# A transformer block with rotating weight tiles: first projection's conditioning blocks in pairs, and a longer delay before a conditioning row's columns are used

## The chip, the core and the metric

The kernel runs on one core of a Trainium2 chip. The metric is the device time of one execution in microseconds (us). TensorE (PE) multiplies, VectorE (DVE) and ScalarE (ACT) work on rows, GpSimd (POOL) and SyncE (SP) issue transfers.

## The reference

The network has two parts in a row on one sequence of 256 tokens with 1024 channels: two layers (attention with an MLP, a recurrent block with an MLP), and behind them a block with three mixers and a mixture of experts. Each sub-layer's input and output are modulated by a conditioning vector `c`. The part that the change touches is the first modulation and the projection behind it:

```python
def ada_modulation(c, w, b):
    mod = jax.nn.silu(c) @ w + b
    shift, scale, gate = jnp.split(mod, 3, axis=-1)
    return shift[:, None, :], scale[:, None, :], gate[:, None, :]
...
        shift, scale, gate = ada_modulation(c, ada_w[i, 0], ada_b[i, 0])
        h = x * (1.0 + scale) + shift
        if i % N_MIXERS == 0:
            y = windowed_gqa(h, attn_w_in[j], attn_w_out[j], attn_sinks[j])
...
        x = layer_norm(DN_ALPHA * x + (1.0 + gate) * y, ln_g[i, 0], ln_b[i, 0])
```

All inputs are float32. `c` is one row of 1024, and each conditioning weight is 1024 by 3072, so a conditioning product is a row times a matrix, and most of its cost is reading the matrix.

## The kernel before, in words

**The stream of weights.** All large matrices of the kernel pass through one list of items, `W` (class `Stream`, L136 on). Each item is a tile of up to 1 MB. Five buffers rotate (`NSTAGE`), SP issues the transfers in the list's order (`load_to`, L194), and an item's buffer is free when its reader is done. There are two kinds of items. A weight (`add`) is split into a high and a low float32r part before use, 1024 columns at a time: ScalarE writes `wh` (L219), VectorE the remainder `wl` (L224); `mm3` (L389 to L393) then multiplies three times, high by high, and each low by the other's high. A filler (`fill`) is a tile of a conditioning matrix with a function that uses it. `W.step()` advances by one item, `W.next(tag)` runs fillers until it comes to the named weight, and `W.drain()` runs the fillers up to the next weight. Each step also issues loads for the next five items and splits for the next weight.

**Orders.** TensorE's instructions in the attention are issued in the order in which the program writes them (`manual_schedule`). The other engines' orders are made when the program is built: an operation goes in when its inputs are reckoned ready, and among those that are ready the one that the program wrote first goes first. On the chip each engine works in its fixed order and waits at an operation whose inputs are late.

**The first projection** (`project`, L1087 to L1119) runs over eight chunks of 128 input channels. For each chunk the weight's 128 rows of 1536 columns are one item ("attn_in", 768 KB, runs of 6 KB), and 18 matmuls add this chunk to six accumulators: keys and values for two halves of the tokens (6 matmuls, two buffers of `gen`, a pool of three, L404) and queries (12 matmuls, `acc`). The chunk's input has to be modulated first. Its 128 shifts and 128 scales come from one filler: `ada0(c)` (L660) reads 1024 rows of two stretches of 128 columns, in runs of 512 bytes, 1 MB in all; eight matmuls (`cS` has silu(c) in one column of 32, L673) leave partial rows in four groups of PSUM partitions, and VectorE copies them to `adaR` (L675). `modulate(c)` (L1075) turns them into two columns with matmuls by a column of ones (L1079, into a buffer of `gen`), VectorE adds the bias (`ab`, L1081), ScalarE scales and shifts the chunk (`v`, L1083), and VectorE splits it into hH and hL (L1084, L1085). In the list blocks and weights alternate. Within chunk c the order is: weight c, the product of block c+1, keys and values of c, `modulate(c + 1)`, queries of c. Behind some chunks stands a piece of another computation (`next(hy)`, the long filters of the second part).

**Rows to columns.** The shifts and scales of the later modulations are made from rows too, but go through memory: `row_cols` (L487) writes the row to DRAM (`flat`, L491) and reads it back as columns (`adaC`, L492), both on POOL's queue, and puts the function that uses the columns on a list with a count of `LAG`:

```python
        GP.dma_start(flat, R[row:64 * n:32, :])
        GP.dma_start(C[:, :n, :], flat.rearrange("(s r) (p k) -> s (r p) k", s=n, k=8).rearrange("s p k -> p s k"))
        W.due.append([LAG, lambda: use(C)])
```

Every `step` begins with `wait_less` (L252), which counts the list down by one and runs a function whose count is below 0. So with `LAG = 2` the function's operations are written at the third step after `row_cols`, with 4 at the fifth. The normalisation behind a sub-layer (`post`, L1350) runs whatever is still listed. The functions are `use` in `ada1` (L571 to L575, operations on `sst` and `ab`) for three modulations, and in `ada2` (L601 to L603, and L610) for the second part.

**The attention's end.** There the first of these rows is finished, and beside it the gate of the attention, whose matrix is four fillers that VectorE multiplies (`adav`, L466 and L468, two operations each). The steps behind `row_cols` are: two gate fillers, the third output weight, two gate fillers, the fourth output weight. Then `gate_sums` (L507) sums the gate over partitions with matmuls into `gen` (L504) and VectorE adds them to the gate (L505). Then come the last products of probabilities and values (`ov`, L1192) and the output projection.

Of the kernel before, what the change touches and what calls it, by code (L numbers as in the profile page):

```python
# [11 lines left out]
F32 = mybir.dt.float32  # L12
# [3 lines left out]
OP = mybir.AluOpType  # L16
# [17 lines left out]
GROUPS = [(0,), (1, 2), (3, 4), (5, 6)]  # L34
RANK = [0, 6, 7, 8, 9, 2, 3, 1, 4, 5, 10, 11, 12, 13]
NSTAGE, NPART, NMORE = 5, 4, 6
LAG = 2
QSCALE = float(HD ** -0.5)


# [94 lines left out]
class Stream:  # L135
# [124 lines left out]
    def next(self, tag, ahead=None):  # L260
        while True:
            got = self.step(ahead)
            if got is not None:
                assert got[0] == tag, (got[0], tag)
                return got[1]
# [15 lines left out]
def tile_model(ctx: ExitStack, tc: tile.TileContext, A, out):  # L281
    nc = tc.nc
    PE, V, SC, GP = nc.tensor, nc.vector, nc.scalar, nc.gpsimd
# [4 lines left out]
    sml = ctx.enter_context(tc.tile_pool(name="sml", bufs=2))  # L288
    rows = ctx.enter_context(tc.tile_pool(name="rows", bufs=4, space=bass.MemoryType.DRAM))

    W = Stream(tc, stage, parts, NSTAGE, 1)
# [14 lines left out]
    def K(name):  # L306
        o, n = OFF[name]
        return csm[:, o:o + n]

    ident = K("ident")  # L310
    one = K("ones")
# [14 lines left out]
    cS = cst.tile([128, 8, 32], F32, name="cS")  # L326
# [6 lines left out]
    csil = cst.tile([128, 3, 8], F32, name="csil")  # L333
# [55 lines left out]
    def mm3(o, a, b, first, last):  # L389
        (ah, al), (bh, bl) = a, b  # L390
        PE.matmul(o, ah, bh, start=first, stop=False)  # L391
        PE.matmul(o, ah, bl, start=False, stop=False)  # L392
        return PE.matmul(o, al, bh, start=False, stop=last)  # L393
# [5 lines left out]
    psC = pes.enter_context(tc.tile_pool(name="psC", bufs=1, space=PSUM))  # L399

    def accb():
        return psA.tile([128, 512], F32, name="acc")

    def gen():  # L404
        return psB.tile([128, 512], F32, name="gen")
# [8 lines left out]
    def finish(job=None):  # L414

        if job is not None:
            FIN["jobs"].append(job)
        if job is None or not FIN["keep"]:
            while FIN["jobs"]:
                FIN["jobs"].pop(0)()  # L420

    def ada_fill(key, cs, wv, c0, n, fin, bank=None, biases=None):
# [4 lines left out]
        def step(kc, last):  # L427
            def fn(t):
# [8 lines left out]
                if last:  # L437
                    R = sml.tile([128, 512], F32, name="adaR", bufs=1)
                    if biases:
                        V.tensor_add(R[:, :n], st["ps"][:, :n], biases())  # L440
                    else:
                        V.tensor_copy(R[:, :n], st["ps"][:, :n])
                    finish(lambda: fin(R))
            return fn
# [32 lines left out]
    def sum_rows(acc, n):  # L477

        ps = gen()
        for g in range(2 * n):  # L480
            PE.matmul(ps[32 * g:32 * g + 32, :], one.to_broadcast([128, 32]), acc[:, 512 * g:512 * g + 512],
                      start=True, stop=True)
        R = sml.tile([128, 512], F32, name="adaR", bufs=1)
        SC.activation(R[:64 * n, :], ps[:64 * n, :], AF.Copy)
        return R

    def row_cols(R, row, n, use):  # L487
# [4 lines left out]
        GP.dma_start(C[:, :n, :], flat.rearrange("(s r) (p k) -> s (r p) k", s=n, k=8).rearrange("s p k -> p s k"))  # L492
        W.due.append([LAG, lambda: use(C)])

# [63 lines left out]
    def biases():  # L558
        return MOD["b5"]
# [76 lines left out]
    def rview(name, idx):  # L636
        return A[name][idx].rearrange("(m p) n -> p m n", p=128)
# [17 lines left out]


    ADA0 = {}
    VCH = ()

    def ada0(c):  # L660
        def fn(t):
            tv = t.rearrange("p (j n) -> p j n", j=8)
            if c in VCH:
                R = sml.tile([128, 256], F32, name="adaQ")
                V.tensor_scalar(R, tv[:, 0, :], csil[:, 0, 0:1], None, op0=OP.mult)
                for j in range(1, 8):
                    V.scalar_tensor_tensor(R, tv[:, j, :], csil[:, 0, j:j + 1], R, op0=OP.mult, op1=OP.add)
                ADA0[c] = R
                return
            ps = psC.tile([128, 512], F32, name="adaps")  # L670
            for j in range(8):
                g = j % 4
                PE.matmul(ps[32 * g:32 * g + 32, :256], cS[:, j, :], tv[:, j, :], start=(j < 4), stop=(j >= 4))  # L673
            R = sml.tile([128, 512], F32, name="adaR", bufs=1)
            V.tensor_copy(R[:, :256], ps[:, :256])  # L675
            ADA0[c] = R

        ap = A["ada_w"][0, 0][:, 0:2048].rearrange("(p j) (s c n) -> c p j s n", j=8, s=2, n=128)[c]
        W.fill("ada", ap, fn)

    wv, wo = rview("attn_w_in", 0), rview("attn_w_out", 0)
    for k in range(8):
        ada0(k)
        W.add("attn_in", wv[:, k, :])
    fl = collect([ADA1[0, 1][0], ADA1[0, 0][3]])
    for m in range(4):
# [354 lines left out]
    def attention():  # L1041
        aes = ExitStack()
        ap = aes.enter_context(tc.tile_pool(name="attn", bufs=1, reuse_waits="tile"))
# [13 lines left out]
        def turn_in(first):  # L1057
            for b in (0,) if first else (1, 2, 3):
                pt = accb()
                for k in range(2):  # L1060
                    for t in range(2):
                        c = 2 * b + k
                        PE.transpose(pt[:, 256 * k + 128 * t:256 * k + 128 * t + 128],
                                     x_nat[:, t, 128 * c:128 * c + 128], ident)
                (SC.copy if b % 2 else V.tensor_copy)(xT[:, 2 * b:2 * b + 2, :],
                                                      pt.rearrange("p (k n) -> p k n", k=2))
            if not first:
                return
            pt = gen()
            PE.transpose(pt[:, 0:16], brow, ident[:16, :16])  # L1070
            pv = pt[:, 0:16].rearrange("p (s k) -> p s k", s=2)
            V.tensor_copy(badd[:, 0], pv[:, 0])
            V.tensor_scalar(badd[:, 1], pv[:, 1], 1.0, None, op0=OP.add)

        def modulate(c):  # L1075
            R = ADA0.pop(c)
            ps = gen()
            for s in range(2):
                PE.matmul(ps[:, s:s + 1], R[:, 128 * s:128 * s + 128], one, start=True, stop=True)  # L1079
            ab = sml.tile([128, 2], F32, name="ab0")  # L1080
            V.tensor_add(ab, ps[:, 0:2], badd[:, :, c])  # L1081
            v = ip.tile([128, 256], F32, name="v0", bufs=2)
            SC.activation(v, xT[:, c, :], AF.Identity, bias=ab[:, 0:1], scale=ab[:, 1:2])  # L1083
            V.tensor_copy(hH[:, c, :], v)  # L1084
            V.tensor_sub(hL[:, c, :], v, hH[:, c, :].bitcast(F32))  # L1085

        def project(hy):  # L1087
            W.step()
            turn_in(True)
            kv = [gen(), gen()]  # L1090
            modulate(0)
            
            qa = [[accb(), accb()], [accb(), accb()]]
            for c in range(8):
                w = W.next("attn_in")
                (qh, ql), (kh, kl) = w.parts

                def rows(ps, t, wh, wl):
                    ts = slice(128 * t, 128 * t + 128)
                    mm3(ps, (hH[:, c, ts], hL[:, c, ts]), (wh, wl), c == 0, c == 7)  # L1100

                if 0 < c < 7:
                    W.step()
                for t in range(2):
                    rows(kv[t], t, kh, kl)
                if c == 0:
                    turn_in(False)
                    W.step()
                if c < 7:
                    modulate(c + 1)  # L1110
                for g in range(2):
                    sl = slice(512 * g, 512 * g + 512)
                    for t in range(2):
                        rows(qa[g][t], t, qh[:, sl], ql[:, sl])
                for _ in range((0, 1, 0, 0, 1, 1, 1, 1)[c]):
                    next(hy)
                if c == 6:
                    nc.sync.dma_start(amask, A["c_amask"])
            return kv, qa  # L1119
# [90 lines left out]

        hy = hy_filters()
        ps, qa = project(hy)
        ies.close()
        aw = aes.enter_context(tc.tile_pool(name="attw", bufs=2, reuse_waits="tile"))
        ADP["pool"] = aes.enter_context(tc.tile_pool(name="adv", bufs=1, reuse_waits="tile"))
        kn = []
        for t in range(2):
            k = aw.tile([128, 4, 128], F32, name="qn", bufs=4)
# [516 lines left out]
    for g in range(4):  # L1735
        p = 64 * (g % 2)
# [348 lines left out]
    with tc.tile_pool(name="rtr", bufs=1, reuse_waits="tile") as rp:  # L2085
# [23 lines left out]
        for t in range(2):  # L2109
            sv = x_nat[:, t, :].rearrange("p (q k) -> p k q", k=8)  # L2110
            for q in range(2):
                ps = gen()
# [38 lines left out]
        m = rp.tile([128, 4, 2], F32, name="rm")  # L2151
# [41 lines left out]
        a, b, c, d = (sv[:, :, j] for j in range(4))  # L2193
# [22 lines left out]
        for j in range(2):  # L2216
            ps = gen()
# [319 lines left out]
```

## Time and profile before

| | us |
|---|---|
| median of 3 runs | 1220.73 (1217.04 to 1220.78) |
| the profiled execution | 1219.98 |
| its span | 1218.2 |

| engine | busy us | share of the span |
|---|---|---|
| TensorE | 1128.1 | 93% |
| VectorE | 771.6 | 63% |
| ScalarE | 552.4 | 45% |
| GpSimd | 104.2 | 9% |

The profile is of one execution. Its span runs from the first instruction to the last; the execution's own time is 1.8 us more. The first projection takes some 60 us of the span, up to 70, and the attention behind it ends near 142. A row of the timeline gives start, duration, engine, line, operation, what it writes and reads, and how long the engine stood before it and for whom. A matmul's end is modelled, so that neighbours overlap: the distance between starts is the better measure.

### The profile page before, as it was taken

The numbers are of one execution on the slowest core, as the hardware profiler recorded it, in microseconds if no ns is written. First come the engines' busy times: TensorE is split into PE (matmuls) and PEld (weight loads), VectorE is DVE, ScalarE is ACT, GpSimd is POOL, SyncE is SP. The second block draws the span as 40 slices with busy tenths as digits, with TensorE's granted clock in tenths as the row PEclk, the third lists the DMA queues.
The fourth block names the chain that finished last, engine by engine and source line by source line (L and its number), as shares of the span: only waits on it lengthen the run. The fifth ranks groups of instructions, "written<-read, shape, count | busy, mean of one in ns | idle before, by whom it ended". The sixth has DMA issues, their size and how long they took to land. (4 is left out here: it accounts for less than half of the span.)

```text
span 1218.2 us, 17320 instructions
## 1 busy us (share of the span) xinstructions
PE 1128.1 (93%) x6610; PEld 822.0 (67%) x6610; DVE 771.6 (63%) x1448; ACT 552.4 (45%) x935; POOL 104.2 (9%) x177
## 2 busy tenths in 40 slices
PE   5999699999989999979999999899999997989884
PEld 3657598988866577558889989899987543334321
DVE  4588688878575786588778879878798511101003
ACT  2456344454467777745345547644656211011101
POOL 6000170000013210010000000100000000000000
PEclk9999889999999999989999999999999899999998
DMA  9988498988694572478779766653346769999993
GB/s 285 327 320 302 175 311 295 337 293 306 205 277 125 168 198 69 143 279 323 261 267 321 270 211 208 209 174 129 100 143 239 284 249 419 417 413 419 420 411 124
DMA packets 147075, 317.58 MB, mean 261 GB/s; under 512 B 8402, under 2 KB 97730, under 8 KB 133672
## 3 DMA queue, kind: packets, MB, share of 16 engines
q1 hardware_dynamic: 139768, 304.17, 69.9%
q0 software_dynamic: 7216, 12.22, 3.2%
q8 instruction: 54, 0.88, 0.3%
q14 instruction: 37, 0.30, 0.1%
HBM read 315.27 MB, written 1.09 MB: 260 GB/s over the span
## 5 line engine op out<-in xcount | busy, mean ns | idle before, releaser
L219 ACT ACTIVATE wh<-stg 128x1024 fp32r<-128x1024 f32 x236 | 241.2, 1042 | 190.2 <-issue 71.9
L224 DVE TENSOR_TENSOR wl<-stg,wh 128x1024 fp32r<-128x1024 f32 x233 | 277.0, 1207 | 75.8 <-ACT wh L219 73.0
L391 PE MATMUL gen<-hH,wh 128*128 128x256 f32 x704 | 198.5, 282 | 4.3 <-ACT hH L851 3.0
L393 PE MATMUL gen<-hH,wl 128*128 128x256 f32 x704 | 197.2, 281 | 5.0 <-DVE wl L224 5.0
L392 PE MATMUL gen<-hL,wh 128*128 128x256 f32 x704 | 196.3, 279 | 1.3 <-DVE hL L855 1.3
L391 PEld LDWEIGHTS gen<-hH,wh 128*128 128x128 f32 x704 | 133.7, 190 | 12.1 <-ACT hH L851 5.7
L393 PEld LDWEIGHTS gen<-hH,wl 128*128 128x128 f32 x704 | 133.8, 190 | 7.9 <-DVE wl L224 7.8
L392 PEld LDWEIGHTS gen<-hL,wh 128*128 128x128 f32 x704 | 133.5, 190 | 3.2 <-POOL zp L1458 1.1
L391 PE MATMUL acc<-wh,mH 128*128 128x512 f32 x256 | 101.3, 396 | 0.0
L393 PE MATMUL acc<-wh,mL 128*128 128x512 f32 x256 | 100.7, 393 | 0.0
L392 PE MATMUL acc<-wl,mH 128*128 128x512 f32 x256 | 100.5, 392 | 0.0
L468 DVE SCALAR_TENSOR_TENSOR adav<-stg,csil,adav 128x1024 f32<-128x1024 f32 (+2 forms) x56 | 79.3, 1415 | 10.2 <-DMA stg<-in_ada_w_dram 9.4
L2423 PE MATMUL mmi<-stg,mhT 128*32 128x512 f32 (+2 forms) x256 | 69.6, 599 | 7.7 <-SPq L2486 3.9
L2395 PE MATMUL mgu<-stg,wh 128*32 128x512 f32 (+2 forms) x256 | 66.6, 648 | 5.9 <-DMA stg<-in_moe_w_up_dram 5.9
L2395 PE MATMUL mgu<-stg,wl 128*32 128x512 f32 (+2 forms) x256 | 65.1, 595 | 7.2 <-DMA stg<-in_moe_w_up_dram 7.2
L2400 DVE SCALAR_TENSOR_TENSOR mhid<-mgu,mws,mhid 128x512 f32<-128x512 f32 x7 | 5.3, 750 | 93.8 <-PE mgu L2395 93.8
L1503 PE MATMUL gen<-xr,bd 128*128 128x256 f32 (+1 forms) x224 | 60.3, 410 | 1.4 <-DVE xr L1479 1.4
L2428 ACT ACTIVATE wh<-mmi 128x512 fp32r<-128x512 f32 x14 | 8.4, 598 | 111.7 <-PE mmi L2423 111.7
L2423 PEld LDWEIGHTS mmi<-stg,mhT 128*32 128x32 f32 (+2 forms) x256 | 20.2, 129 | 54.5 <-issue 36.2
L2429 DVE TENSOR_TENSOR wl<-mmi,wh 128x512 fp32r<-128x512 f32 x14 | 9.7, 692 | 74.0 <-ACT wh L2428 74.0
L391 PEld LDWEIGHTS acc<-wh,mH 128*128 128x128 f32 x256 | 48.1, 188 | 11.7 <-ACT mH L1310 0.8
L393 PEld LDWEIGHTS acc<-wh,mL 128*128 128x128 f32 x256 | 48.1, 188 | 11.0 <-issue 0.8
(597 smaller groups left out, 2160.0 us busy)
## 6 DMA issues: line engine op xcount, KB each, us to landing
stg<-in_ada_w_dram SPq DMA_DIRECT2D x72, 1024.0 KB, 6.1
stg<-in_mlp_w_dram SPq DMA_DIRECT2D x64, 1024.0 KB, 6.5
stg<-in_moe_w_up_dram SPq DMA_DIRECT2D x32, 1024.0 KB, 16.3
stg<-in_moe_w_gate_dram SPq DMA_DIRECT2D x32, 1024.0 KB, 15.2
stg<-in_moe_w_down_dram SPq DMA_DIRECT2D x32, 1024.0 KB, 18.8
stg<-in_w_in_dram SPq DMA_DIRECT2D x20, 1024.0 KB, 5.4
stg<-in_rnn_w_in_dram SPq DMA_DIRECT2D x12, 1024.0 KB, 6.3
stg<-in_attn_w_in_dram SPq DMA_DIRECT2D x8, 768.0 KB, 10.4
```

The lines of the kernel that those rows point to most:

```text
L219: nc.scalar.activation(h, t[:, sl], AF.Copy)
L224: sub()
L391: PE.matmul(o, ah, bh, start=first, stop=False)
L392: PE.matmul(o, ah, bl, start=False, stop=False)
L393: return PE.matmul(o, al, bh, start=False, stop=last)
L468: V.scalar_tensor_tensor(acc, tv[:, j, :], col[:, k:k + 1], acc, op0=OP.mult, op1=OP.add)
L1503: PE.matmul(pv[c0:c1, q, :], BD[g % 2][:, q, d, o:o + c1 - c0], xr[g][:, kt, :], start=(i == 0), stop=True, skip_group_check=True)
L2395: PE.matmul(ps[sl], gx[c][:, k, o + sl.start:o + sl.stop], t[:, 512 * k:512 * k + 512], start=first, stop=last)
L2400: V.scalar_tensor_tensor(hid, got[1], WS[w], hid, op0=OP.mult, op1=OP.mult)
L2423: PE.matmul(ps[h][sl], hT[:, 2 * c + k, sl], t[:, 1024 * k + 512 * h:1024 * k + 512 * h + 512], start=c == 0 and k == 0, stop=c == 1 and k ...
L2428: SC.activation(yH[:, h, :], ps[h], AF.Copy)
L2429: V.tensor_sub(yL[:, h, :], ps[h], yH[:, h, :].bitcast(F32))
```

## The change

The blocks of chunks 0 and 1 stay as they are. Those of 2 and 3, 4 and 5, 6 and 7 are read in pairs: one item has the shifts of both chunks and one the scales, in runs of 1 KB; both products go to one PSUM tile, and one copy of 512 columns serves both chunks. In the list the two items of a pair stand in front of the pair's two weights. In chunks 1, 3 and 5 the first product stands behind the first three of the 12 query matmuls, the second behind the next three, and both `modulate` follow; chunks 2, 4 and 6 have neither. `LAG` becomes 4. A branch that no chunk took (`VCH`) is gone.

```diff
@@ -34,7 +34,7 @@
 GROUPS = [(0,), (1, 2), (3, 4), (5, 6)]
 RANK = [0, 6, 7, 8, 9, 2, 3, 1, 4, 5, 10, 11, 12, 13]
 NSTAGE, NPART, NMORE = 5, 4, 6
-LAG = 2
+LAG = 4
 QSCALE = float(HD ** -0.5)
 
 
@@ -655,32 +655,51 @@
 
 
     ADA0 = {}
-    VCH = ()
 
     def ada0(c):
+
         def fn(t):
             tv = t.rearrange("p (j n) -> p j n", j=8)
-            if c in VCH:
-                R = sml.tile([128, 256], F32, name="adaQ")
-                V.tensor_scalar(R, tv[:, 0, :], csil[:, 0, 0:1], None, op0=OP.mult)
-                for j in range(1, 8):
-                    V.scalar_tensor_tensor(R, tv[:, j, :], csil[:, 0, j:j + 1], R, op0=OP.mult, op1=OP.add)
-                ADA0[c] = R
-                return
             ps = psC.tile([128, 512], F32, name="adaps")
             for j in range(8):
                 g = j % 4
                 PE.matmul(ps[32 * g:32 * g + 32, :256], cS[:, j, :], tv[:, j, :], start=(j < 4), stop=(j >= 4))
             R = sml.tile([128, 512], F32, name="adaR", bufs=1)
             V.tensor_copy(R[:, :256], ps[:, :256])
-            ADA0[c] = R
+            ADA0[c] = [R[:, 128 * s:128 * s + 128] for s in range(2)]
 
         ap = A["ada_w"][0, 0][:, 0:2048].rearrange("(p j) (s c n) -> c p j s n", j=8, s=2, n=128)[c]
         W.fill("ada", ap, fn)
 
+    def ada0_pair(c):
+
+        st = {}
+
+        def fn(q, t):
+            tv = t.rearrange("p (j n) -> p j n", j=8)
+            if q == 0:
+                st["ps"] = psC.tile([128, 512], F32, name="adaps")
+            ps = st["ps"]
+            for j in range(8):
+                g = j % 4
+                PE.matmul(ps[32 * g:32 * g + 32, 256 * q:256 * q + 256], cS[:, j, :], tv[:, j, :], start=(j < 4), stop=(j >= 4))
+            if q == 0:
+                return
+            R = sml.tile([128, 512], F32, name="adaR", bufs=1)
+            V.tensor_copy(R, ps)
+            for m in range(2):
+                ADA0[c + m] = [R[:, 256 * s + 128 * m:256 * s + 128 * m + 128] for s in range(2)]
+
+        ap = A["ada_w"][0, 0][:, 0:2048].rearrange("(p j) (s c n) -> s c p j n", j=8, s=2, n=256)
+        for q in range(2):
+            W.fill("ada", ap[q, c // 2], partial(fn, q))
+
     wv, wo = rview("attn_w_in", 0), rview("attn_w_out", 0)
     for k in range(8):
-        ada0(k)
+        if k < 2:
+            ada0(k)
+        elif k % 2 == 0:
+            ada0_pair(k)
         W.add("attn_in", wv[:, k, :])
     fl = collect([ADA1[0, 1][0], ADA1[0, 0][3]])
     for m in range(4):
@@ -1076,7 +1095,7 @@
             R = ADA0.pop(c)
             ps = gen()
             for s in range(2):
-                PE.matmul(ps[:, s:s + 1], R[:, 128 * s:128 * s + 128], one, start=True, stop=True)
+                PE.matmul(ps[:, s:s + 1], R[s], one, start=True, stop=True)
             ab = sml.tile([128, 2], F32, name="ab0")
             V.tensor_add(ab, ps[:, 0:2], badd[:, :, c])
             v = ip.tile([128, 256], F32, name="v0", bufs=2)
@@ -1099,19 +1118,22 @@
                     ts = slice(128 * t, 128 * t + 128)
                     mm3(ps, (hH[:, c, ts], hL[:, c, ts]), (wh, wl), c == 0, c == 7)
 
-                if 0 < c < 7:
-                    W.step()
                 for t in range(2):
                     rows(kv[t], t, kh, kl)
                 if c == 0:
                     turn_in(False)
                     W.step()
-                if c < 7:
-                    modulate(c + 1)
+                    modulate(1)
                 for g in range(2):
                     sl = slice(512 * g, 512 * g + 512)
                     for t in range(2):
                         rows(qa[g][t], t, qh[:, sl], ql[:, sl])
+                        if c in (1, 3, 5) and g + t == 0:
+                            W.step()
+                    if c in (1, 3, 5) and g == 0:
+                        W.step()
+                        modulate(c + 1)
+                        modulate(c + 2)
                 for _ in range((0, 1, 0, 0, 1, 1, 1, 1)[c]):
                     next(hy)
                 if c == 6:
```

## Rows read from the trace of the kernel before

**Rows 1.** The page, its first part: busy time, share of the span, instructions.

```profile
PE 1128.1 (93%) x6610; PEld 822.0 (67%) x6610; DVE 771.6 (63%) x1448; ACT 552.4 (45%) x935; POOL 104.2 (9%) x177
```

**Rows 2.** Windows: stretch, length, busy us (instructions) by engine, PEclk, DMA share, GB/s.

```profile
25.28:66.00 40.72, 40.18 (x248) 27.75 (x247) 22.83 (x51) 15.70 (x22) 1.28 (x3) 1.00 1.07 336
...
81.00:120.00 39.00, 36.74 (x182) 23.98 (x182) 33.56 (x67) 26.27 (x63) 1.01 (x2) 1.00 0.86 330
```

**Rows 3.** TensorE's waits from 25.28 to 66 us: total, times, longest.

```profile
PE gen L1079 <- DVE adaR L675: 0.5, 1, 0.5
```

**Rows 4.** Timeline of chunk 3: start, us, engine, line, operation, [idle before it].

```profile
40.64 1.07 PE L673 MATMUL adaps<-stg,cS 128*32 128x256 f32 x16
...
41.77 0.42 DVE L675 COPY adaR<-adaps 128x256 f32<-128x256 f32 x1 [2.27 <-PE adaps L673]
...
43.12 0.50 PE L1079 MATMUL gen<-csm,adaR 128*128 128x1 f32 x4
...
43.49 0.48 PE L391 MATMUL acc<-wh,hH 128*128 128x512 f32 x1
...
43.66 0.16 DVE L1081 TENSOR_TENSOR ab<-gen,badd 128x2 f32<-128x2 f32 x1 [1.46 <-PE gen L1079]
...
44.88 0.43 DVE L1085 TENSOR_TENSOR hL<-v,hH 128x256 fp32r<-128x256 f32 x1
```

**Rows 5.** Timeline of chunk 2, the copy of the product and its neighbours.

```profile
35.01 1.83 DVE L224 TENSOR_TENSOR wl<-stg,wh 128x1024 fp32r<-128x1024 f32 x2 [2.10 <-ACT wh L219]
...
37.23 0.61 PE L1079 MATMUL gen<-csm,adaR 128*128 128x1 f32 x4 [0.54 <-DVE adaR L675]
```

**Rows 6.** Timeline of the attention's end, a row's columns and the gate.

```profile
112.81 0.66 DVE L442 COPY adaR<-adaps 128x512 f32<-128x512 f32 x1
...
115.57 2.60 DVE L468 SCALAR_TENSOR_TENSOR adav<-stg,csil,adav 128x1024 f32<-128x1024 f32 x2
...
119.60 0.75 POOL L492 DMA_DIRECT2D adaC<-flat  x1 [5.23 <-DMA flat<-adaR]
...
120.92 1.89 PE L1192 MATMUL gen<-PT,vN 128*128 128x256 f32 x8
...
125.42 0.17 DVE L571 TENSOR_TENSOR sst<-adaC,adb 128x8 f32<-128x8 f32 x1 [4.88 <-DMA adaC<-flat]
...
125.58 0.69 DVE L505 SCALAR_TENSOR_TENSOR gate<-gen,gate 128x512 f32<-128x512 f32 x1
...
126.33 3.78 PE L1192 MATMUL gen<-PT,vN 128*128 128x256 f32 x8 [3.52 <-DVE gate L505]
```

**Rows 7.** Windows behind that wait, columns as above.

```profile
125.00:128.00 3.00, 1.67 (x4) 1.41 (x5) 2.58 (x8) 0.00 (x0) 0.00 (x0) 0.53 1.03 408
...
130.00:132.00 2.00, 2.00 (x6) 1.56 (x5) 0.69 (x1) 1.55 (x2) 0.54 (x1) 0.50 1.05 367
```

**Rows 8.** Windows of short and long runs; GB/s in 40 slices, 730 to 760.

```profile
40.00:56.00 16.00, 16.00 (x110) 11.04 (x109) 8.52 (x20) 6.59 (x8) 0.00 (x0) 1.00 1.14 334
...
56.00:70.00 14.00, 14.00 (x71) 9.82 (x70) 10.60 (x39) 6.52 (x13) 0.00 (x0) 1.00 1.02 418
...
GB/s 0 0 0 0 64 309 388 384 376 333 350 354 219 23 20 0 5 145 343 384 385 212 277 388 415 243 11 0 0 66 266 382 388 292 26 0 11 194 378 388
```

**Rows 9.** Timeline of chunk 1: the next weight's split and the product.

```profile
26.44 1.06 ACT L219 ACTIVATE wh<-stg 128x1024 fp32r<-128x1024 f32 x1 [0.19 <-DMA stg<-in_attn_w_in_dram]
...
28.22 1.07 PE L673 MATMUL adaps<-stg,cS 128*32 128x256 f32 x16
```

**Rows 10.** Second MLP: VectorE's wait for columns from 572 to 590, TensorE's row behind.

```profile
DVE ss L601 <- DMA adaC<-flat: 5.0, 1, 5.0
...
584.51 0.38 PE L393 MATMUL gen<-hH,wl 128*128 128x256 f32 x1 [0.43 <-DVE wl L224]
```

**Rows 11.** A wait in the attention, and the window around it.

```profile
89.20 1.13 PE L1022 MATMUL gen<-hh,fwdf 128*128 128x512 f32 x2 [1.57 <-ACT qT L1149]
...
80.00:90.00 10.00, 8.43 (x46) 3.88 (x47) 7.59 (x20) 7.46 (x23) 0.00 (x0) 1.00 1.00 395
```

## Prediction

> **What bounds the kernel now.** I read the page first: TensorE is busy for 93% of the span [rows 1], and the chain that ended last only names the final normalisation, so the question is whether TensorE is also the bound in the two places that the change touches. For the first projection the windows answer it: from 25.28 to 66 us TensorE is busy for 40.18 of 40.72 us, with the transfers saturated beside it at 336 GB/s [rows 2]. Both look like a limit; the view of the waits decides. In that stretch TensorE waits once, for 0.5 us, and for VectorE's copy, never for a transfer [rows 3]. So the transfers keep just ahead, and what counts there is the length of TensorE's own sequence. The attention behind it is much the same, 36.74 of 39 us busy [rows 2].
>
> The sequence of one chunk is seen at chunk 3 [rows 4]: the conditioning product (16 records, 1.07 us) is followed by six key and value matmuls, and under these VectorE copies the product, so that the row-to-column matmuls at 43.12 find it ready. 0.37 us later the query matmuls start, and they cover the sum `ab` and what follows from it. Nothing waits. In chunk 2 the copy stood on VectorE behind the two splits of the next weight, ended late, and TensorE lost those 0.54 us [rows 5].
>
> The second place is the use of a conditioning row's columns, which the LAG delays. Its dearest wait is in the attention [rows 6]: the product's row is copied at 112.81, its way out and back takes until 125.42 (the transfer back is issued at 119.60), and VectorE stands still for the last 4.88 us of it. Behind the use stands the gate's sum (L505), which frees the PSUM buffer that TensorE needs: TensorE loses 3.52 us there. [...]
>
> **The change, part by part.** I sum on TensorE's sequence in the projection, because its waits have no cover there.
>
> *Removed.* With the products moved to the middle of the odd chunks, a copy no longer competes with splits that start at the chunk's beginning; I count the 0.54 us of chunk 2 as gained, and with the matmul pitch that it broke 0.7.
>
> *Moved, no cost.* Products and row-to-column matmuls are as many as before (16 product records for each of eight blocks, 4 for each chunk). Six copies of 0.42 us become three of 0.66 [rows 4, 6], 0.5 us less on VectorE, which is off the path. TensorE changes between kinds of work about as often.
>
> *Added: the copy's wait.* In a pair the second product is followed at once by the first `modulate`. No key and value matmuls stand between them, so the copy loses its cover: 0.06 us from the product's end to the copy (at chunk 3: 41.71 to 41.77), 0.66 for 512 columns, 0.06 to the matmul. That is 0.8 us. The bounds: 0.5 with the old narrow copy, and 2.0 if one split of 1.2 us stands ahead of it.
>
> *Added: the buffer's wait.* Two of the three buffers of `gen` hold keys and values, so the second `modulate` of a pair takes the buffer of the first and waits for its `ab`. From the first matmul to `ab` it is 0.54 us, `ab` takes 0.16, 0.06 back [rows 4]: 0.76, where the next work came after 0.37. That is 0.4 us, with bounds 0.2 and 0.8. What is queued behind both waits is the rest of the chunk's query matmuls, and six of them (six times 0.23 us) still cover hH and hL of the next chunk, which end 1.65 us after `ab` starts (45.31 against 43.66).
>
> Sum: three pairs at 0.8 and 0.4 make 3.6, a lost pitch at each (0.05) takes it to 3.75, less 0.7: **3.0 us more**, within 1.4 (three times 0.7, less 0.7) and 7.7 (three times 2.8, less 0.7).
>
> *The 1 KB runs.* In the saturated stretch from 40 to 56 us a block of 512-byte runs and its weight arrive at 334 GB/s; long runs arrive at 418 [rows 8]. A chunk's 1.835 MB take 5.49 us, its 0.786 MB of weight 1.88 of them, so a block takes 3.6 us (290 GB/s). The second network's projection loads blocks with 1 KB runs, and there the saturated slices show 384 to 388 [rows 8]: 2.7 us. Six blocks get 5.4 us of transfer time back. I credit none of it: TensorE waits for no transfer here [rows 3]. [...]
>
> *Are the blocks there in time?* Both blocks of the first pair are now due in chunk 1. Before, TensorE began that chunk at 28.22, and the weight behind block 2 had landed by 26.44 [rows 9]. In the new order block 2 (2.7 instead of 3.6 us) and block 3 in place of that weight (2.7 instead of 1.9) end near 26.4, or at 28.2 without any gain from the runs. The second product is due near 32. Cover: 4 to 6 us; were it gone, each late microsecond would cost one.
>
> *Queues.* SP issues as many transfers, two in a row where one and a weight alternated; a buffer of the five is freed half a chunk later, which that cover takes. POOL's queue keeps its two transfers per row: only the use moves.
>
> *LAG 4.* What stands on VectorE is not in the program's order: the row's copy, written at the last product's step, stands at 112.81 behind operations of later steps. An operation is placed where its inputs are reckoned ready. The use at 125.42 already stands behind the pair of `adav` operations at 115.57 [rows 6], and these belong to the last step ahead of the gate. Four steps put the use in front of that very pair, two put it a weight and a fill earlier; in both cases the gate's sum is written after it. So nothing passes it: I take 0. The bounds are 0 and minus 6.4 (3.5 of wait, and half of the 5.7 us from 126.3 to 132 for the clock). The other waits for these columns are worth little even where they go: in the second MLP a stand of 5 us on VectorE cost TensorE 0.43 [rows 10].
>
> The profiled execution took 1219.98 us, 0.75 below the median of the runs (1220.73). 1219.98 and 3.0 are 1223.0, so against the median I forecast 1223.7.
>
> **The rivals.**
> *The gate's sum passes the use.* If the new order of transfers shifts the reckoning, the sum may stand first. For it: use and sum are 0.16 us apart on VectorE. Against it: nothing in the written order favours the sum. 3.0 less 6.4 is -3.4: 1217.3.
> *The copy stands behind splits.* Ends on the slower side. Its place is the end of the second product; it decides where the next weight's splits (1.83 us [rows 5]) stand ahead of the copy and its weight lands less than some 3 us before that product ends. Then each pair loses up to 1.9 more, 5.7 in all: 1229.4. For it: this happened in chunk 2. Against it: the copy now comes 4 us after the chunk's start, where the splits become free to run.
> *The transfers do set the pace* and TensorE's sequence is slack: then the 5.4 us come off and the waits hide, 1215.3. Against it is the single wait of [rows 3].
> *The clock falls in the new waits.* A wait of 1.57 us at 89.20 left it at 1.00 [rows 11], and the new ones are shorter; I give it no chance of its own.
>
> **How the numbers follow.** A measurement of this kernel tells about 0.3% (3.7 us) from no change. The forecast gets 0.45; its bounds reach across 3.7, so 0.28 of it is no change and 0.17 slower. The passing gate gets 0.22 (0.13 no change, 0.09 faster), the copy behind splits 0.13 (slower), the transfers' pace 0.10 (faster), and other shifts of order 0.10 (0.05 faster, 0.02, 0.03). Together 0.24 faster, 0.43 the same, 0.33 slower. The range runs from 1216.0, just below the passing gate, to 1229.5; the forecast's own is 1222.1 to 1228.4.
>
> **What would show it.** In the profile of after: three waits of TensorE for the copy near 0.8 us and three for `ab` near 0.4, at chunks 1, 3 and 5; the projection's end 3 us later; the transfers idle earlier; the 3.5 us wait for the gate and the half clock behind it still there. The forecast is wrong if TensorE's wait for the gate is gone, if waits for transfers appear at a pair, or if the projection ends sooner.

## The result, and the profile after

The change makes the kernel slower. Over 20 runs of each the median goes from 1218.10 to 1225.47 us; the ratio of the runs is 1.0064, with a 95% interval from 1.0047 to 1.0081, or 7.8 us (5.7 to 9.9). The forecast had said 3.0 us more and had called no change the likeliest outcome.

The page of after shows the same load as [rows 1]: busy times hardly move.

```profile
PE 1129.7 (93%) x6610; PEld 819.9 (67%) x6610; DVE 770.3 (63%) x1445; ACT 551.8 (45%) x935; POOL 104.0 (9%) x177
```

The two profiled executions differ by only 2.6 us (1222.58 against 1219.98), and that is an accident of the part behind the attention, which neither edit touches: over the fourteen profiles of this document it takes anything from 1065 to 1072 us. Two instructions make better marks than the end of the span: the last long-filter matmuls behind the projection, and the transposes of x behind the attention's normalisation, which in every run come after the same wait of 3.1 us for ScalarE. In the timeline of before (TensorE only) they stand at 70.37 and 148.02:

```profile
70.37 2.84 PE L998 MATMUL gen<-hw,ha 64*128 64x512 f32 x6
...
148.02 1.16 PE L842 MATMUL gen<-csm,xnat 128*128 128x128 f32 x8 [3.09 <-ACT xnat L891]
```

and in that of after at 80.86 and 155.70:

```profile
80.86 2.84 PE L1017 MATMUL gen<-hw,ha 64*128 64x512 f32 x6
...
155.70 1.97 PE L861 MATMUL gen<-csm,xnat 128*128 128x128 f32 x8 [3.08 <-ACT xnat L910]
```

So the projection takes 10.5 us more, and the attention gives 2.8 back. The 7.7 that are left agree with the 7.8 of the ratio; from the second mark to the end this execution of after happened to be 5.1 us quicker (1065.1 against 1070.2). A second profile of each kernel (in the table below) gives 9.9 and 7.8 us at the two marks.

**The projection.** TensorE's waits from 25.28 to 81 us, where [rows 3] showed one of 0.5 us:

```profile
PE gen L1098 <- DVE adaR L689: 2.4, 3, 0.8
PE gen L1098 <- DVE ab L1100: 2.0, 3, 1.2
```

That is 4.4 us, six waits in three pairs, and none for a transfer. It is less than half of the 10.5. The rest is in the granted clock (windows of after, columns as in [rows 2]; the clock is the third number from the end):

```profile
36.30:39.60 3.30, 3.30 (x9) 2.61 (x8) 1.37 (x3) 0.63 (x1) 0.00 (x0) 0.51 1.03 294
49.90:53.30 3.40, 3.40 (x9) 2.67 (x10) 3.07 (x8) 2.21 (x4) 0.00 (x0) 0.52 0.97 335
67.00:73.50 6.50, 6.50 (x16) 4.13 (x15) 3.26 (x10) 1.44 (x3) 0.00 (x0) 0.50 0.95 360
```

Behind each pair TensorE is busy without a gap, at a clock of 0.51, 0.52 and 0.50, for 3.3, 3.4 and 6.5 us. What a full clock would have saved I estimate from these at 3.30 x 0.49, 3.40 x 0.48 and 6.50 x 0.50, together 6.5 us. In before the clock was 1.00 all through this stretch [rows 2, 8].

The third pair shows how it begins (timeline of chunk 5 in after, lines of TensorE and VectorE that answer to [rows 4]):

```profile
61.73 1.07 PE L685 MATMUL adaps<-stg,cS 128*32 128x256 f32 x16
...
62.86 0.69 DVE L689 COPY adaR<-adaps 128x512 f32<-128x512 f32 x1 [2.81 <-PE adaps L685]
...
63.47 1.82 DVE L224 TENSOR_TENSOR wl<-stg,wh 128x1024 fp32r<-128x1024 f32 x2
63.61 0.61 PE L1098 MATMUL gen<-csm,adaR 128*128 128x1 f32 x4 [0.81 <-DVE adaR L689]
65.21 0.15 DVE L1100 TENSOR_TENSOR ab<-gen,badd 128x2 f32<-128x2 f32 x1
...
65.41 0.61 PE L1098 MATMUL gen<-csm,adaR 128*128 128x1 f32 x4 [1.20 <-DVE ab L1100]
...
66.92 0.63 PE L392 MATMUL acc<-wl,hH 128*128 128x512 f32 x1
67.35 0.63 PE L393 MATMUL acc<-wh,hL 128*128 128x512 f32 x1
```

The second product, 0.81 us of standing, four one-column matmuls, 1.20 us of standing, four more: a microsecond later the large matmuls start 0.43 us apart where they had been 0.23 apart. `ab` is late because two splits of the next weight (1.82 us) stand between the copy and it.

**The attention's end** (timeline of after, answering to [rows 6]):

```profile
122.82 0.68 DVE L442 COPY adaR<-adaps 128x512 f32<-128x512 f32 x1
...
132.61 1.89 PE L1214 MATMUL gen<-PT,vN 128*128 128x256 f32 x8
...
135.26 0.17 DVE L571 TENSOR_TENSOR sst<-adaC,adb 128x8 f32<-128x8 f32 x1 [6.41 <-DMA adaC<-flat]
...
135.82 0.69 DVE L505 SCALAR_TENSOR_TENSOR gate<-gen,gate 128x512 f32<-128x512 f32 x1
...
136.57 2.00 PE L1214 MATMUL gen<-PT,vN 128*128 128x256 f32 x8 [2.07 <-DVE gate L505]
```

The use of the columns still stands ahead of the gate's sum. But TensorE comes to this point 11.7 us later than before (132.61 against 120.92), and the columns only 9.8 later (135.26 against 125.42). The wait shrinks from 3.52 to 2.07 us, and the clock stays up behind it: the eight matmuls take 2.00 us instead of 3.78, and a window around the wait and what follows it is at 1.00, where the windows behind it in before [rows 7] were at 0.53 and 0.50:

```profile
118.00:142.00 24.00, 21.23 (x103) 14.86 (x102) 15.14 (x28) 12.74 (x23) 2.42 (x4) 1.00 0.85 302
```

So 1.5 us of the wait are saved, and by the matmuls' half speed in before, as an estimate, some 2.8 (half of the 5.7 us from 126.3 to 132). Ahead of the wait 1.2 us are lost (11.7 against the 10.5 of the first mark), and of the 3.1 that this leaves, 2.8 are seen at the second mark.

### The profile page after: what moved, and what is told of

Its sections match the earlier page's. It is cut to its first block, busy times and chain, and to the rows that moved or that the text cites. A ratio compares the mean times of both kernels' runs of the same rounds, so it can differ in the third digit from the quotient of the medians.

```text
span 1220.8 us, 17317 instructions
## 1 busy us (share of the span) xinstructions
PE 1129.7 (93%) x6610; PEld 819.9 (67%) x6610; DVE 770.3 (63%) x1445; ACT 551.8 (45%) x935; POOL 104.0 (9%) x177
## 5 line engine op out<-in xcount | busy, mean ns | idle before, releaser
L468 DVE SCALAR_TENSOR_TENSOR adav<-stg,csil,adav 128x1024 f32<-128x1024 f32 (+2 forms) x56 | 79.2, 1415 | 10.4 <-DMA stg<-in_ada_w_dram 9.6
L392 PEld LDWEIGHTS acc<-wl,mH 128*128 128x128 f32 x256 | 48.1, 188 | 10.3 <-DVE wl L224 0.6
```

The lines of the kernel that those rows point to most:

```text
L468: V.scalar_tensor_tensor(acc, tv[:, j, :], col[:, k:k + 1], acc, op0=OP.mult, op1=OP.add)
```

## The experiments

Theory: the pairs' two waits, and the clock that falls in them, make the difference. Rivals: the later use of the columns, the run length, or the small products themselves. All kernels are built on one of the two; the marks are the starts named above. Each ratio is to runs of before made beside it, whose median lay between 1214.61 and 1218.10 us, so the ratios can be compared and the medians can't.

| kernel | filters | transposes | median | ratio to before, 95% |
|---|---|---|---|---|
| before; a second profile | 70.37; 69.23 | 148.02; 145.44 | | |
| after; a second profile | 80.86; 79.13 | 155.70; 153.20 | 1225.47 | 1.0064 (1.0047 to 1.0081) |
| pairs_covered | 72.40 | 147.09 | 1219.58 | 1.0020 (0.9991 to 1.0050) |
| uncovered_singles | 76.95 | 151.36 | 1223.02 | 1.0042 (1.0017 to 1.0068) |
| copy_wait_only | 74.93 | 149.95 | one run | |
| ab_wait_only | 74.05 | 148.23 | one run | |
| second_bank | 74.91 | 149.27 | 1219.48 | 1.0027 (0.9996 to 1.0057) |
| products_thrice | 74.65 | 151.04 | one run | |
| pairs_512 | 82.23 | 156.92 | 1227.07 | 1.0078 (1.0049 to 1.0108) |
| lag_alone | 69.63 | 145.66 | 1217.78 | 0.9997 (0.9970 to 1.0024) |
| gate_first | 70.27 | 141.45 | 1212.35 | 0.9979 (0.9962 to 0.9997) |
| covered_gate_first | 72.79 | 145.13 | 1213.93 | 0.9989 (0.9964 to 1.0014) |

### The same pairs with cover: pairs_covered

```diff
                 for t in range(2):
                     rows(kv[t], t, kh, kl)
+                    if c in (1, 3, 5) and t == 0:
+                        W.step()
+                        W.step()
...
+                if c in (2, 4, 6):
+                    modulate(c + 1)
                 for g in range(2):
...
                         if c in (1, 3, 5) and g + t == 0:
-                            W.step()
-                    if c in (1, 3, 5) and g == 0:
-                        W.step()
-                        modulate(c + 1)
-                        modulate(c + 2)
+                            modulate(c + 1)
```

> The changed kernel, with the same pairs, the same 1 KB runs and LAG = 4, but both products behind the first three key and value matmuls, six matmuls between the second product and the first modulate, and the second modulate in the next chunk. Theory (waits and clock): no wait for adaR or ab above 0.2 us in chunks 1 to 6, granted clock 1.00 from 25 to 70, the projection's end back from 81 to 70 us, and the time 5 to 10 us below the changed kernel, that is 3 us below to 2 us above the kernel before. Rival (the small products themselves, two close together, lower the clock): about 3 us of half clock behind each pair without any wait, the end near 75, 3 to 6 us above before. Rival (the blocks are not in time): waits for stg at the products.

The window and the waits of this kernel (25.28 to 66, and 25.28 to 78 us):

```profile
25.28:66.00 40.72, 38.13 (x240) 26.74 (x239) 21.68 (x46) 15.20 (x22) 0.61 (x2) 1.00 0.99 346
```

```profile
PE gen L393 <- DVE hL L1104: 1.5, 2, 1.2
PE gen L392 <- DVE wl L224: 0.8, 1, 0.8
```

The clock is up (1.00), both waits are gone, and of the 10.5 us 8.5 are back. The last 2 are new waits of 2.3 us for VectorE's splits, which I had not foreseen: one of 1.2 us, between large matmuls, left the clock at 1.00. With the same pairs and the same 1 KB runs the kernel is at best level with before, so the pairs as such bring nothing here.

### Waits without pairs: uncovered_singles

```diff
-                if 0 < c < 7:
-                    W.step()
                 for t in range(2):
                     rows(kv[t], t, kh, kl)
+                if 0 < c < 7:
+                    W.step()
```

> The kernel before, with its single blocks and LAG = 2, but in chunks 1 to 6 the product stands behind the key and value matmuls, directly ahead of modulate, so that the copy has no cover. Theory (short waits beside the small products let the granted clock fall, whether paired or not): six waits for adaR of about 0.54 us (0.06, 0.42, 0.06), more where a split stands ahead of the copy, half clock behind some of them, and 4 to 12 us above before. Rival (the clock falls only where copy wait and buffer wait follow each other, as in a pair): the waits alone, less the 0.7 us of chunk 2, so 2 to 3 us above before with the clock at 1.00 up to 70 us.

Timeline of TensorE in chunks 5 and 6, with VectorE ahead of the sixth wait, and two windows:

```profile
57.97 0.61 PE L1079 MATMUL gen<-csm,adaR 128*128 128x1 f32 x4 [0.55 <-DVE adaR L675]
...
64.37 1.81 DVE L224 TENSOR_TENSOR wl<-stg,wh 128x1024 fp32r<-128x1024 f32 x2
...
66.11 0.41 DVE L675 COPY adaR<-adaps 128x256 f32<-128x256 f32 x1
...
66.57 0.61 PE L1079 MATMUL gen<-csm,adaR 128*128 128x1 f32 x4 [1.97 <-DVE adaR L675]
```

```profile
52.00:66.00 14.00, 12.05 (x74) 7.43 (x72) 10.92 (x24) 6.17 (x9) 0.00 (x0) 1.00 1.05 379
67.00:71.00 4.00, 4.00 (x12) 3.14 (x12) 0.88 (x3) 0.60 (x1) 0.00 (x0) 0.57 1.03 418
```

Five waits of 0.55 us cost their length and no more (the clock from 25.28 to 66 us is at 1.00); the sixth, with two splits ahead of the copy, is 1.97 us long, and behind it the clock is down (0.57). Both theories were half right: it took no pair here, and 0.55 us alone didn't do it.

### One of the two waits at a time: copy_wait_only, ab_wait_only, second_bank

In copy_wait_only the second modulate of a pair goes to the next chunk:

```diff
+                if c in (2, 4, 6):
+                    modulate(c + 1)
...
                         modulate(c + 1)
-                        modulate(c + 2)
```

> The changed kernel, with the second modulate of a pair moved into the next chunk, behind its keys and values: the three waits for the copy stay (0.8 us each), the three for ab go. Theory (it is the whole stretch of small work and waits from the second product to the last column that lets the clock fall, 1.07, 0.81, 0.61, a second wait, 0.61): the stretch is shorter by more than 0.8 us, the granted clock stays at 1.00 from 25 to 70, and the projection ends near 73 us, 2.4 us of waits behind before. Rival (one wait of 0.8 us beside small products is enough): about 3 us of half clock behind each pair, the end at 77 to 79.

In ab_wait_only it is pairs_covered with both modulates together again:

```diff
-                if c in (2, 4, 6):
-                    modulate(c + 1)
...
                         if c in (1, 3, 5) and g + t == 0:
                             modulate(c + 1)
+                            modulate(c + 2)
```

> The changed kernel, with both products behind the first three key and value matmuls and six matmuls between them and the two modulates, which follow each other as in the change: the waits for the copy go, those for ab stay. Theory (whole stretch): 0.61, a wait of 0.25 to 1.2, 0.61 are too short a stretch, the clock stays at 1.00 but for a place where a split of 1.2 or 1.8 us stands ahead of ab, and the projection ends at 71 to 74 us. Rival (the wait for ab is what lets the clock fall): half clock behind each pair, the end at 75 to 79.

The waits of copy_wait_only (25.28 to 78 us), then those of ab_wait_only:

```profile
PE gen L1098 <- DVE adaR L689: 2.4, 3, 0.8
PE gen L391 <- DVE hH L1103: 1.7, 2, 1.0
```

```profile
PE gen L1098 <- DVE ab L1100: 1.2, 3, 0.7
```

Neither has a half clock behind a pair (1.00 from 30 to 81 us in both). copy_wait_only ends 2 us later than I expected, for waits of 1.7 us for hH that I had left out. ab_wait_only ends where expected, with one surprise, at chunk 0 (timeline and window):

```profile
24.72 0.61 PE L1098 MATMUL gen<-csm,adaR 128*128 128x1 f32 x4 [1.44 <-DVE adaR L668]
```

```profile
25.00:28.50 3.50, 3.50 (x11) 2.82 (x12) 0.94 (x3) 0.60 (x1) 0.96 (x2) 0.53 1.06 391
```

At the same place pairs_covered waited 1.75 us, and its clock stayed at 1.00:

```profile
24.46 0.61 PE L1098 MATMUL gen<-csm,adaR 128*128 128x1 f32 x4 [1.75 <-DVE adaR L668]
```

At this place the length of the wait didn't decide: three more profiles waited longer than 1.44 us there (1.52 in products_thrice, 1.69 in the second profile of after, 1.95 in second_bank) and kept the clock at 1.00. second_bank is the smallest repair, the changed kernel with one line different:

```diff
-            ps = gen()
+            ps = psC.tile([128, 512], F32, name="adaps") if c in (3, 5, 7) else gen()
```

> The changed kernel, with the second modulate of each pair in the PSUM tile of the product (free after the copy) instead of a buffer of gen: the waits for ab go, those for the copy stay at 0.8 us, and both modulates still follow each other ahead of the query matmuls. Theory (the two waits together with the small work let the clock fall; without the second it holds): clock at 1.00 from 25 to 70, the projection ends at 73 to 74, and the time is 5 to 8 us below the changed kernel, 0 to 3 above before. Rival (two modulates in a row behind the copy's wait are enough): half clock behind the pairs, the end at 77 to 79.

Timeline of its third pair, and the window:

```profile
60.68 0.61 PE L1098 MATMUL gen<-csm,adaR 128*128 128x1 f32 x4 [0.81 <-DVE adaR L689]
61.15 0.58 PE L1098 MATMUL adaps<-csm,adaR 128*128 128x1 f32 x4
```

```profile
25.28:66.00 40.72, 36.51 (x231) 24.47 (x231) 19.64 (x42) 14.84 (x21) 0.76 (x2) 1.00 0.96 327
```

The copy's waits are all there, the clock is up (1.00), and the projection ends 5.95 us earlier than in the first profile of the changed kernel. The waits it removed are 2.0 us and hH's new ones 1.7, so nearly all of this is clock. In the timed runs it is 1.0027 where after was 1.0064, a gain of 4.5 us, a little under what I expected; the two intervals overlap, so the profile carries this more than the time does.

### Small work without a wait: products_thrice

```diff
-            for j in range(8):
+            for j in list(range(8)) * (3 if c in (2, 4, 6) else 1):
```

> The kernel before, with the products of chunks 2, 4 and 6 issued three times over (the same values each time), so that TensorE does 3.2 us of small matmuls in a row and waits for nothing. Theory (the clock falls for small work in a stretch, whether TensorE stands or not): half clock behind some of the three places. Rival (TensorE has to stand still as well): the granted clock stays at 1.00 from 25 to 76. The repeated work itself costs 3 times 2.1 us either way, so the projection ends at 76 to 77 with the clock up, at 79 or more with a fall.

The first of the three places in its timeline (chunk 1), and the window over all three:

```profile
27.63 2.80 PE L673 MATMUL adaps<-stg,cS 128*32 128x256 f32 x48
```

```profile
25.28:66.00 40.72, 40.47 (x325) 27.55 (x323) 21.00 (x44) 14.79 (x20) 0.64 (x2) 1.00 1.05 331
```

The rival holds: 2.80 us of small products without a stand left the clock at 1.00. My theory had to be narrowed: in these places TensorE had to stand as well. (A repeat cost 0.87 us, not 1.07, so the end came earlier than I had expected.)

### Is a fall a property of the program? after_again, before_again

> The changed kernel once more, for a second profile. If the clock falls at fixed places, there is half clock behind all three pairs again (3.3, 3.4 and 6.5 us), the projection's last large product of the filters starts near 80.9 and the transposes behind the normalisation near 155.7. If a fall at a given wait is a matter of the execution, one or more of the three is missing, and the start near 80.9 moves by 1.5 us or more for each.

Windows of the second profile of after:

```profile
36.30:39.60 3.30, 3.30 (x16) 2.68 (x16) 1.30 (x3) 0.63 (x1) 0.00 (x0) 1.00 1.04 319
49.90:53.30 3.40, 3.40 (x13) 2.69 (x12) 2.33 (x4) 2.12 (x3) 0.00 (x0) 0.76 0.97 314
67.00:73.50 6.50, 6.50 (x19) 4.93 (x18) 3.11 (x9) 0.42 (x1) 0.00 (x0) 0.62 0.96 358
```

The pairs' waits are the same (2.4 and 2.0 us), but behind the first pair the clock stayed up, and the filters start 1.73 us earlier. So a fall was here in part a matter of the execution.

> The kernel before once more, for a second profile. If the clock falls at fixed places of a program, the projection again runs at 1.00 and ends near 70 us, the wait for the gate is 3 to 3.6 us with some 5 us of half clock behind it, and the transposes behind the attention's normalisation start within 1 us of 148.0. If a fall at a given wait is a matter of the execution, the half clock behind the gate's wait is missing or of another length, and that start moves by 2 us or more.

Timeline of its second `ov` product:

```profile
124.78 3.66 PE L1192 MATMUL gen<-PT,vN 128*128 128x256 f32 x8 [3.10 <-DVE gate L505]
```

Here the clock fell in both profiles (0.53 and 0.50 from 125 to 128), for a shorter time in the second (130 to 132 is at 1.00 there). The profiles of pairs and of uncovered products together, by what TensorE did around the small matmuls of chunks 1 to 6:

| arrangement | places | half clock behind |
|---|---|---|
| copy's wait and `ab`'s wait (after twice, pairs_512) | 9 | 8 |
| copy's wait of 0.8 alone (copy_wait_only, second_bank) | 6 | 0 |
| `ab`'s wait alone (ab_wait_only) | 3 | 0 |
| neither (pairs_covered, covered_gate_first) | 6 | 0 |
| single product, wait of 0.55 | 5 | 0 |
| single product, wait of 1.97 | 1 | 1 |

What the rows don't separate is the number of waits from their sum. A single 0.81 us kept the clock six times, and 0.81 with another 0.25 behind it, the second pair, lost it in all three profiles; but that sum, 1.06 us, also lies above every single wait that kept the clock in this table, and no run has one wait of that length at these places.

### Run length: pairs_512

```diff
-                ADA0[c + m] = [R[:, 256 * s + 128 * m:256 * s + 128 * m + 128] for s in range(2)]
+                ADA0[c + m] = [R[:, 256 * m + 128 * s:256 * m + 128 * s + 128] for s in range(2)]
...
-        ap = A["ada_w"][0, 0][:, 0:2048].rearrange("(p j) (s c n) -> s c p j n", j=8, s=2, n=256)
+        ap = A["ada_w"][0, 0][:, 0:2048].rearrange("(p j) (s c n) -> c p j s n", j=8, s=2, n=128)
         for q in range(2):
-            W.fill("ada", ap[q, c // 2], partial(fn, q))
+            W.fill("ada", ap[c + q], partial(fn, q))
```

> The changed kernel with its order and its LAG, but each item of a pair is one chunk's block in 512-byte runs, as before. Theory (run length plays no part, the transfers are ahead either way): within 2 us of the changed kernel, with the waits for adaR at 0.8 us three times and a projection that ends near 81 us. Rival (the 1 KB runs carry part of the time): waits for stg of 2 us and more at the second or third pair, and 3 to 8 us above the changed kernel.

TensorE's waits from 25.28 to 78 us:

```profile
PE gen L1098 <- DVE ab L1100: 3.0, 3, 1.5
PE gen L1098 <- DVE adaR L689: 2.4, 3, 0.8
```

None for `stg`. The ratios stand 1.7 us apart, within their intervals, and the waits for `ab` are 1.0 us longer. Run length plays no part in the time that these runs could show.

### The columns and the gate: lag_alone, gate_first, covered_gate_first

```diff
-LAG = 2
+LAG = 4
```

> The kernel before with LAG = 4 and nothing else. Theory (the pairs' waits, and the granted clock that falls in them, make the whole difference; LAG adds nothing): within 2 us of before, the projection ends near 70 us, no wait of TensorE for adaR or ab above 0.6 us, and the wait for the gate in the attention stays between 3 and 5 us. Rival (the later use is what costs, at the attention's end or in the MLPs): 5 to 9 us slower than before with the projection as before.

The time is that of before, the wait for the gate 3.0 us. And in the changed kernel LAG does nothing at all: with 2 in place of 4 it has the same instructions in the same order with the same waits on every engine (read from the two programs; it was not run).

gate_first and covered_gate_first do what the longer LAG did not: they put the use behind the gate, on before and on pairs_covered (a LAG of 6 by itself was not run).

```diff
-LAG = 2
+LAG = 6
...
+                with ExitStack() as es:
+                    if idx == 1:
+                        es.enter_context(tc.issue_after(TABLE["ol"].ins))
+                    V.tensor_add(tmp[:, 0], C[:, 0], adb[:, idx, 0])
...
-                V.tensor_sub(oL[:, sl, :], pv, oH[:, sl, :].bitcast(F32))
+                TABLE["ol"] = V.tensor_sub(oL[:, sl, :], pv, oH[:, sl, :].bitcast(F32))
```

> The kernel before, its projection untouched; in the attention the use of the first row's columns is put on VectorE behind the last split of the output of the products with the probabilities (oL), so that the gate's sums don't stand behind it (a LAG of 6 for all rows, which writes it late enough). Theory: the wait of 3.5 us for the gate goes, the clock stays at 1.00 from 120 to 132, the attention ends 3 to 6 us earlier than before, and the time is 2 to 6 us below before. Rival (the next one that is late takes its place: a weight's split, the gate's row from memory, or the columns themselves, which the normalisation behind needs): the wait moves, and the time is within 2 us of before.

> The kernel with covered pairs, with the use of the first row's columns behind the last split as in gate_first. If the two are independent, its time is that of pairs_covered less what gate_first gains, less the part of the gate's wait that pairs_covered had lost already (1.9 us there, 3.5 before): 0 to 4 us below before. Rival (no gain left): as pairs_covered, 1 to 4 us above before.

Timeline of the attention's end in gate_first, and the window:

```profile
120.19 0.69 DVE L505 SCALAR_TENSOR_TENSOR gate<-gen,gate 128x512 f32<-128x512 f32 x1 [0.19 <-PE gen L504]
...
120.84 3.62 PE L1195 MATMUL gen<-PT,vN 128*128 128x256 f32 x16
...
125.74 0.16 DVE L574 TENSOR_TENSOR sst<-adaC,adb 128x8 f32<-128x8 f32 x1
```

```profile
120.00:132.00 12.00, 12.00 (x53) 9.74 (x52) 8.33 (x16) 3.54 (x5) 1.54 (x3) 1.00 1.05 384
```

All sixteen matmuls run through, nobody waits for the columns, and the transposes start 6.6 and 4.0 us earlier than in the two profiles of before. The timed runs show 2.6 (0.4 to 4.6): less, and how often the clock falls at this wait in the runs that have no profile stays open. gate_first is the one version here that beats both kernels. On covered pairs the same edit comes out at 0.9989, within what was expected, and no better than on before.

## Why the prediction was right or wrong

- **The bound** (TensorE's own sequence, transfers just ahead): right. No run shows a wait for a block, and pairs_512 takes the run length out of the time. In after the transfers come to rest for a while from 58 to 62 us (49 and 29 GB/s), well before the projection's end, as said. What part of that the 1 KB runs have was not shown.
- **The copy's wait**, 0.8 us three times: right, 0.81 each.
- **The lost copy of chunk 2**: its 0.54 us wait is gone, as said. But it was a matter of the execution: the second profile of before has no wait there, and lag_alone and gate_first, with the same projection, have 0.4 and 0.6 us. So the 0.7 us could be counted only against the one profile.
- **The buffer's wait**, 0.4 us three times, at most 0.8: wrong in size. It is 0.60, 0.25 and 1.20, or 2.05 instead of 1.2. The rival had splits stand ahead of the copy; in the first and third pair they stood one place further, between the copy and `ab`, where I had costed VectorE as free.
- **The clock**: this is the step that failed. "The clock falls in the new waits ... I give it no chance of its own", because one wait of 1.57 us had left it at 1.00 and the new ones are shorter. That wait stood among large matmuls. Here two waits stand among narrow products (32 columns of weights) and one-column matmuls, and the clock fell behind 8 of 9 such pairs: 6.5 us in the first profile, more than twice the whole forecast. In the two profiles of after no wait in the pairs is above 1.20 us, and the clock fell behind five of the six. With waits of 2.43 and 2.05, the lost pitch of 0.15 and less 0.7, the sum is 3.9, and with the clock 10.4, against 10.5 measured where the sum had 3.0.
- **LAG at 0**: right, for the reason given. Also right is that the sum behind the use is what TensorE waits for: gate_first puts it ahead, and the wait goes.
- **"The 3.5 us wait for the gate and the half clock behind it still there"**: wrong. I had summed the projection and the attention as if the one did not move the other. TensorE's delay hid part of the columns' trip, and with a wait of 2.07 us (1.30 in the second profile) the clock held at 1.00. That gave 2.8 us back; the 5.7 us of half clock, of which the forecast's bound for LAG takes half, are those of [rows 6, 7]. Over the twelve profiles in which TensorE stood for the gate, the clock fell behind the four longest waits (2.15 to 3.52 us; the eight matmuls behind took 3.62 to 3.78 us) and held behind the eight others (1.30 to 2.07; they took 1.99 or 2.00). The shortest that lost it is in products_thrice:

```profile
130.45 3.62 PE L1192 MATMUL gen<-PT,vN 128*128 128x256 f32 x8 [2.15 <-DVE gate L505]
```

- **The number**: 1225.5 lies inside the range, and inside the forecast's own, and that is partly luck. The forecast stood on a median of three runs, 1220.73, where twenty gave 1218.10: the number missed by 1.8 us, but the change, 7.8 us where 3.0 was said, is at the very end of the sum's bounds (1.4 to 7.7). And two terms that the sum put at nothing, 6.5 us of half clock in the projection and 2.8 us given back in the attention, stood against each other. The chances were less good: slower had 0.33 and no change 0.43.

## What to carry to other kernels

Count a wait on TensorE twice: by its length, and by what TensorE does around it. A short wait between large matmuls cost its length here (up to 2.07 us, with the clock at 1.00); two of them among one-column and narrow matmuls, three times, cost here another 6.5 us of half clock, so put large matmuls between a product, its copy and what reads the copy, or give the second reader a PSUM tile of its own (pairs_covered and second_bank, both at 1.00). And place marks behind the edit: a span of 1220 us hid 5 of the 7.7 us that two starts showed. Where a term rests on a wait in one profile, such as chunk 2's, take a second profile.

## What was not expected of the hardware

A fall of the granted clock was not fixed by the program here: with the same waits of TensorE in the pairs (2.4 and 2.0 us), one execution of after lost the clock behind the first pair (0.51) and the next did not (1.00), and at chunk 0 a wait of 1.44 us lost it (0.53, ab_wait_only) where one of 1.75 kept it (1.00, pairs_covered). And narrow matmuls alone did not lose it: 48 records of them in 2.80 us without a stand left it at 1.00 (products_thrice).
